# A hybrid decoder layer on one core: where the output projection ends, where the DeltaNet inverse's matmuls stand in the queue, which banks the gates use, and how GLA's output products are ordered

## The chip, the core and the metric

The kernel runs on one core of one Trainium2 chip. The core has five engines that work side by side, each with its own queue of instructions taken in order: PE (TensorE, matrix products), DVE (VectorE), ACT (ScalarE), POOL (GpSimd) and SP (SyncE, which here only issues transfers). Products land in PSUM, which has eight banks of 128 x 512 numbers. The metric is the device time of one execution in microseconds (us); lower is better.

## The reference

One layer of a decoder trunk, in float32, with 512 tokens behind 16 learned meta tokens and 2048 columns. The normalised input goes through one projection, whose columns are shared out to three token mixers; their outputs are gated, laid side by side and projected back. The mixers are a gated DeltaNet (6 heads of 128), GLA, a gated linear attention (5 heads, keys of 64, values of 128), and a forgetting attention, "fox" (5 heads of 128).

```python
h = concatenate([meta, x]);  proj = rms_norm(h, norm_w) @ w_in      # 528 x 7585
# DeltaNet, per chunk of 64 tokens: a_mat is strictly lower triangular
sol = triangular_solve(eye + a_mat, rhs, lower=True, unit_diagonal=True)
u, w = sol[..., :128], sol[..., 128:]
v_new = u - w @ s;  o = (q * exp(g)) @ s + qk @ v_new
s = s * g_last + k_dec.T @ v_new
# GLA, per chunk
o = (q * exp(g)) @ s + attn @ v;  s = g_last[:, None] * s + k_dec.T @ v
# both: o = rms(o) * w * silu(z);  fox: softmax(q k / sqrt(d) + c_t - c_s) v * silu(z)
o = concatenate([o_dn, o_gla, o_fox])[512 tokens]
y = x + o @ w_out                                                   # 2048 x 2048
out = rms_norm(y, final_norm_w)
```

## The kernel before, in words

**Exact splitting.** The two projections use TensorE's float32r form. Every operand is cut in two (`split`, L144 and L145: a cast hi on ScalarE, the rest lo = raw - hi on VectorE), and each product is three matmuls: hi hi, hi lo, lo hi. Weights come in pieces of 128 x 1024 (`load_half`: a load on SP's queue, then the split). The pool wp holds two buffers of each of raw, hi and lo, so that at most two pieces are under way, and a third waits until TensorE has finished with the first. The pool hp holds 32 tiles, first for the split input (xh, xl), at the end for the split outputs of the mixers (oh, ol), for weights kept back (wlh, wll) and for the final norm's weights (fw).

**PSUM.** Two pools of four banks each: psb (tag b) for the projections' accumulators, psm (tag m) for the mixers' small products.

**Order.** The program is written mixer by mixer, but a planner with its own costs merges everything into one fixed order for each engine; splits have high priority. So in the trace the mixers' small products stand among the input projection's matmuls (pp, L168: 128 x 128 weights against 264 or 256 tokens).

The four places that the change touches:

- *Gates.* 64 matmuls (L314) over the input's 16 row blocks give the narrow columns of all gates, for two halves of the tokens, in two accumulators pgate0 and pgate1 taken from psb. What follows adds two row halves and stores them in misc (L319 to L321).
- *The inverse.* DeltaNet works in two groups of three heads. `dn_inverse` inverts the 64 x 64 unit triangles of a group. The 32 x 32 diagonal blocks go by DMA into ab, one block in each of 51 partitions; thirty substitution steps of a multiply and an add on VectorE (L456, L458) invert them; POOL masks twice (L459, L461); a DMA on ScalarE's queue writes the result out (sc2, L464), two more read it back in another layout (iv at L467, xm at L469), and VectorE transposes (L471, L472). Then come 24 small matmuls pm (L478), a copy to m1 (L480), 48 small matmuls pl (L485, L486), and from them the next size up (pn L506, pu L511).
- *GLA's output.* `gla_pair` treats two heads (the last call one). For each head e and each block b of 128 tokens a product of 128 rows (at with vt, L769) and one of 64 rows (qd with the state ss, L770; head 0 uses rows 0 to 63, head 1 rows 64 to 127) add up in the same columns of the accumulator pgo. In the trace one such float32 product is two passes.
- *The output projection and the final norm.* The weight w_out has four column quarters cc of 512 and eight pieces kp, each for two of the sixteen heads i. For cc from 0 to 3 the first seven pieces are multiplied into four accumulators pa, one for each block tb of 128 tokens; for cc below 3 they are added to the residual at once (acc). The eighth piece of every quarter (heads 14 and 15) is kept back (`load_last`, rawl, wlh, wll) and multiplied in a last stage: for tb from 0 to 3 and for cc in the order 3, 0, 1, 2 six matmuls (pz, or pa for quarter 3), an add on VectorE (L972), a square with its sum on ScalarE (L974), and a multiply by fw on POOL (L976) for all but quarter 2. After a block's four quarters come the root (L978 to L980), the scaling of the quarters by ScalarE or VectorE (L984, L986, L988) and the writes, by SP's queue for even quarters and by ScalarE's for odd ones (L990).

Of the kernel before, what the change touches and what calls it, by code (L numbers as in the profile page):

```python
# [8 lines left out]
F32 = mybir.dt.float32  # L9
# [4 lines left out]
AF = mybir.ActivationFunctionType  # L14
ALU = mybir.AluOpType
# [3 lines left out]
P = 128  # L19
D = 2048  # L20
KT = D // P
NM = 16
S = 512
T = NM + S
HT = T // 2
NB = S // P
# [51 lines left out]
def tile_hybrid_trunk(ctx, tc, xT, xtok, mtok, w_gate, w_in, w_out, consts, lmask, fin_w, out, dbg=None):  # L78
    nc = tc.nc
# [19 lines left out]
    V, A, G, PE = nc.vector, nc.scalar, nc.gpsimd, nc.tensor  # L99
# [34 lines left out]
    def load_half(src, name):  # L134
        raw = wp.tile([P, 1024], F32, tag="raw", name=f"raw{name}")
        nc.sync.dma_start(out=raw, in_=src)
# [20 lines left out]
    def part(name, n=512):  # L157
        return hp.tile([P, T], F32R, tag="x", name=name)[:, :n]

    xh, xl = [], []  # L160
    rstd = cst.tile([P, T], F32, name="rstd")

    def inproj_part(ps, parts, k0, n, hi, lo, m=P):
        for j in range(n):
            k = k0 + j
            for wt, xx in ((hi, xh), (hi, xl), (lo, xh)):
                for p_, (t0, nt) in zip(ps, parts):
                    PE.matmul(p_[:, :nt], wt[:, j * m : (j + 1) * m], xx[k][:, t0 : t0 + nt],  # L168
                              start=(k == 0 and wt is hi and xx is xh),
                              stop=(k == KT - 1 and wt is lo))  # L170

    def inproj_begin(key, meta=True, first=0):
        b = BLOCK_OF[key]
# [69 lines left out]
    for b in range(5):  # L243
        r = NM if b == 4 else P
# [48 lines left out]
    zs = {}  # L293
# [13 lines left out]


    misc = cst.tile([64, T], F32, name="misc")
    pgate = [psb.tile([P, 512], F32, tag="b", name=f"pgate{a}") for a in range(2)]  # L310
    for k in range(KT):
        for xx in (xh, xl):
            for a in range(2):
                PE.matmul(pgate[a][:, :HT], wg[k // 8][:, k % 8, :], xx[k][:, a * HT : (a + 1) * HT],  # L314
                          start=(k == 0 and xx is xh), stop=(k == KT - 1 and xx is xl))
# [120 lines left out]
    def dn_inverse(g, st):  # L436
        an, anm = st["an"], st["anm"]
# [28 lines left out]
        xc, uc, m1, l1 = (iv[:, i] for i in range(4))  # L466
# [8 lines left out]
        for n in range(NN):  # L475
            for q in range(2):
                lo_, hi_ = slice(64 * q, 64 * q + 32), slice(64 * q + 32, 64 * q + 64)
                PE.matmul(pm[lo_, n, :], an[hi_, n, lo_], uc[hi_, n, :], start=True, stop=True)  # L478
# [160 lines left out]
    def gla_pair(p):  # L639
        R = P if p < 2 else 64  # L640
        ne = 2 if p < 2 else 1
# [121 lines left out]
            ss.append(sn)  # L763
        po = [psm.tile([P, 512], F32, tag="m", name=f"pgo{p}{e}") for e in range(ne)]
        for e in range(ne):
            rr = slice(64 * e, 64 * e + 64)
            for b in range(NB):
                bs = slice(b * P, (b + 1) * P)
                PE.matmul(po[e][:, bs], at[:, e * NB + b, :], vt[:, e, bs], start=True, stop=False)  # L769
                PE.matmul(po[e][:, bs], qd[rr, bs], ss[b][rr, :], start=False, stop=True)  # L770
# [123 lines left out]
    for h in range(FOX_HEADS):  # L894
        dump(f"ofx{h}", zs["fz", h])


    heads = [("dz", h) for h in range(DN_HEADS)] + [("gz", h) for h in range(GLA_HEADS)] \
        + [("fz", h) for h in range(FOX_HEADS)]
# [9 lines left out]
    def mms(p_, hi, lo, i, tb, first, last):  # L909
        s = slice(tb * P, (tb + 1) * P)  # L910
        oh, ol = oparts[i]
        for n, (o_, w_) in enumerate(((oh, hi), (oh, lo), (ol, hi))):
            PE.matmul(p_, o_[:, s], w_, start=(first and n == 0), stop=(last and n == 2))  # L913

    LAST = 14
    halves = lambda w: [[t[:, j * 512 : (j + 1) * 512] for t in w] for j in range(2)]
    acc, wl = {}, {}

    def load_last(c):
        raw = wp.tile([P, 1024], F32, tag="raw", name=f"rawl{c}")  # L920
        nc.sync.dma_start(out=raw, in_=w_out[c, LAST // 2])
        r = []
        for j in range(2):
            hi, lo = part(f"wlh{c}{j}"), part(f"wll{c}{j}")
            split(raw[:, j * 512 : (j + 1) * 512], hi, lo)
            r.append((hi, lo))
        return r

    for i in range(LAST):
        split_o(i)  # L930
    for cc in range(4):
        pa = [psb.tile([P, 512], F32, tag="b", name=f"pa{cc}{tb}") for tb in range(4)]
        for kp in range(LAST // 2):
            w = halves(load_half(w_out[cc, kp], f"o{cc}_{kp}"))
            for j in range(2):
                i = 2 * kp + j
                for tb in range(4):
                    mms(pa[tb], *w[j], i, tb, i == 0, cc < 3 and i == LAST - 1)
            if cc == 3 and kp % 2 and kp < 6:
                c = kp // 2  # L940
                wl[c] = load_last(c)
        for tb in range(4):
            if 4 * cc + tb < 11:
                a = zp.tile([P, S], F32, tag="zs", name=f"acc{cc}{tb}")
            else:
                a = six.tile([P, S], F32, tag="six", name=f"acc{cc}{tb}")
            nc.scalar.dma_start(out=a, in_=xtok[tb * P : (tb + 1) * P, cc * 512 : (cc + 1) * 512])
            if cc < 3:
                V.tensor_tensor(out=a, in0=a, in1=pa[tb], op=ALU.add)
            acc[tb, cc] = a  # L950
        if cc == 0:
            for i in range(LAST, KT):
                split_o(i)
    wl[3] = halves(load_half(w_out[3, LAST // 2], "l3"))
    fw = []
# [4 lines left out]
    ss = wk.tile([P, 4, 5], F32, tag="fss", bufs=1, name="fss")  # L960
    rr = wk.tile([P, 4], F32, tag="frs", bufs=1, name="frs")
    for tb in range(4):
        for cc in (3, 0, 1, 2):
            a = acc[tb, cc]
            cuts = 2 if (tb, cc) == (3, 2) else 1
            for n in range(cuts):
                c = slice(512 // cuts * n, 512 // cuts * (n + 1))
                p_ = pa[tb] if cc == 3 else psm.tile([P, 512], F32, tag="m", name=f"pz{tb}{cc}{n}")
                for j in range(2):
                    hi, lo = wl[cc][j]  # L970
                    mms(p_[:, c], hi[:, c], lo[:, c], LAST + j, tb, cc < 3 and j == 0, j == 1)
                V.tensor_tensor(out=a[:, c], in0=a[:, c], in1=p_[:, c], op=ALU.add)  # L972
                sq = row(f"sqf{tb}{cc}{n}")
                A.activation(sq[:, c], a[:, c], AF.Square, accum_out=ss[:, tb, cc + 2 * n : cc + 2 * n + 1])  # L974
            if cc != 2:
                G.tensor_tensor(out=a, in0=a, in1=fw[cc], op=ALU.mult)  # L976
# [4 lines left out]
        for cc in (3, 0, 1, 2):  # L981
# [64 lines left out]
```

## Time and profile before

| | |
|---|---|
| time, median of 3 runs | 1046.04 us (1045.03 to 1049.08) |
| profiled execution | 1048.64 us, of which the trace's span is 1046.9 us |
| TensorE busy | 97% of the span, 7787 matmul passes |
| VectorE, ScalarE, POOL busy | 55%, 39%, 13% |
| mean granted TensorE clock | 0.991 |
| memory traffic | 98.74 MB read, 5.05 MB written |

Rows of the profile have this form: line, engine, operation, out<-in by the program's names, partitions x elements, and "x" the count; times are in microseconds unless marked ns. What stands in brackets at the end of a row is how long the engine sat idle before it, and what ended that. PEclk is the clock that the throttle granted to TensorE (1.00, or 9 in the page's row of tenths, is full speed). Matmuls are pipelined: the distance from one start to the next, not the length of a row, is what a matmul costs.

### The profile page before, as it was taken

Reading aid. Unit: us, or ns where it says so; the run is one execution under the profiler, and the core shown is the slowest. Engines: PE = TensorE matmul, PEld = TensorE weight load, DVE = VectorE, ACT = ScalarE, POOL = GpSimd, SP = SyncE. Lnnn points to the kernel's source line nnn. Section 1 sums busy time; section 2 is a strip of 40 time slices with the busy share of each in tenths; the row PEclk is TensorE's granted clock in tenths of the full one; section 3 lists DMA queues with packets and bytes.
Section 4 is the critical chain, followed back from the end, with each engine's and each line's share of the span. In section 5 each row is a group of like instructions: output and inputs, shape, how many; then the busy total and the mean of one; then the engine's idle time right before and its main releaser. Section 6 shows DMA issues by size and latency. Waiting matters only on the chain.

```text
span 1046.9 us, 19027 instructions
## 1 busy us (share of the span) xinstructions
PE 1019.8 (97%) x7787; PEld 914.5 (87%) x7787; DVE 574.8 (55%) x1251; ACT 410.7 (39%) x895; POOL 134.9 (13%) x137
## 2 busy tenths in 40 slices
PE   9999999999999999999999999999999999999994
PEld 7899999989999888899989878898989888888883
DVE  6366868855567972334828274455444474332437
ACT  6643533343455333244344443333323262222234
POOL 0021312220213131000100010110101010000014
PEclk9999999999999998999999999999999999999998
DMA  9613222223222322222212122222222263222424
GB/s 351 233 48 127 82 89 92 99 77 108 89 69 82 96 102 77 69 77 73 78 42 67 46 87 74 94 72 86 89 84 87 86 204 126 93 82 100 141 81 160
DMA packets 42347, 105.15 MB, mean 100 GB/s; under 512 B 10589, under 2 KB 13917, under 8 KB 42260
## 3 DMA queue, kind: packets, MB, share of 16 engines
q1 hardware_dynamic: 26848, 90.23, 24.6%
q10 hardware_dynamic: 15412, 13.70, 4.5%
q8 instruction: 61, 1.00, 0.4%
q14 instruction: 26, 0.21, 0.1%
HBM read 98.74 MB, written 5.05 MB: 99 GB/s over the span
## 4 chain that ended last, share of the span: by engine, by line
PE 54%; DVE 3%; ACT 1%; issue 1%; DMA 0%; DVEq 0%
PE pp L168 29%; PE pa L913 15%; PE pss L708 1%; PE pgo L770 1%; PE pfo L863 1%; PE pgo L769 1%; PE pfa L831 1%; PE pz L913 1%; DVE acc L988 1%; PE pfx L846 1%; ACT sqf L974 0%; PE pfd L832 0%; PE pfo L866 0%; DVE acc L986 0%; PE pgk L660 0%
## 5 line engine op out<-in xcount | busy, mean ns | idle before, releaser
L168 PE MATMUL pp<-xh,whi 128*128 128x264 f32 (+2 forms) x1456 | 378.5, 312 | 0.9 <-DVE vg L278 0.8
L168 PE MATMUL pp<-xh,wlo 128*128 128x264 f32 (+2 forms) x1456 | 376.8, 311 | 0.0
L168 PE MATMUL pp<-xl,whi 128*128 128x264 f32 (+2 forms) x1456 | 376.2, 310 | 0.0
L168 PEld LDWEIGHTS pp<-xh,whi 128*128 128x128 f32 x1456 | 244.5, 190 | 16.0 <-issue 1.4
L168 PEld LDWEIGHTS pp<-xl,whi 128*128 128x128 f32 x1456 | 245.2, 190 | 14.4 <-issue 1.4
L168 PEld LDWEIGHTS pp<-xh,wlo 128*128 128x128 f32 x1456 | 245.4, 190 | 13.3 <-issue 0.3
L145 DVE TENSOR_TENSOR wlo<-raw,whi 128x1024 fp32r<-128x1024 f32 x110 | 136.4, 1240 | 124.6 <-ACT whi L144 123.8
L144 ACT CAST whi<-raw 128x1024 fp32r<-128x1024 f32 x110 | 115.3, 1049 | 202.2 <-PE pp L168 181.1
L913 PE MATMUL pa<-whio,ol 128*128 128x512 f32 x224 | 88.0, 393 | 0.0
L913 PE MATMUL pa<-wloo,oh 128*128 128x512 f32 x224 | 87.9, 393 | 0.0
L913 PE MATMUL pa<-whio,oh 128*128 128x512 f32 x224 | 79.1, 396 | 0.0
L145 DVE TENSOR_TENSOR wloo<-rawo,whio 128x1024 fp32r<-128x1024 f32 x28 | 34.6, 1236 | 75.2 <-ACT whio L144 75.1
L144 ACT CAST whio<-rawo 128x1024 fp32r<-128x1024 f32 x28 | 29.4, 1049 | 93.7 <-PE pa L913 60.1
L913 PEld LDWEIGHTS pa<-whio,ol 128*128 128x128 f32 x224 | 42.1, 188 | 9.9
L913 PEld LDWEIGHTS pa<-wloo,oh 128*128 128x128 f32 x224 | 42.1, 188 | 9.5
L913 PEld LDWEIGHTS pa<-whio,oh 128*128 128x128 f32 x224 | 42.0, 188 | 9.2
L287 POOL TENSOR_SCALAR stc<-cv 128x528 f32<-128x528 f32 (+1 forms) x18 | 28.3, 1572 | 165.3 <-DVE cv L361 142.5
L361 DVE SCALAR_TENSOR_TENSOR cv<-pb,cpk,cv 128x528 f32<-128x528 f32 (+1 forms) x54 | 40.8, 755 | 0.6
L976 POOL TENSOR_TENSOR acc<-acc,fw 128x512 f32<-128x512 f32 x12 | 15.7, 1335 | 170.9 <-ACT sqf L974 170.9
L278 DVE TENSOR_TENSOR pb<-pp,rstd 128x264 f32<-128x264 f32 (+1 forms) x36 | 13.8, 424 | 26.2 <-PE pp L168 26.1
L456 DVE TENSOR_TENSOR ot<-ab 51x30 f32<-51x30 f32 (+14 forms) x60 | 20.3, 339 | 3.3 <-POOL stc L287 1.7
L458 DVE TENSOR_TENSOR ab<-ab,ot 51x30 f32<-51x30 f32 (+14 forms) x60 | 20.6, 343 | 1.5
(380 smaller groups left out, 1304.2 us busy)
## 6 DMA issues: line engine op xcount, KB each, us to landing
raw<-in_w_in SPq DMA_DIRECT2D x110, 512.0 KB, 3.2
rawo<-in_w_out SPq DMA_DIRECT2D x28, 512.0 KB, 3.2
xt<-in_xtok SPq DMA_DIRECT2D x8, 512.0 KB, 9.1
acc<-in_xtok ACTq DMA_DIRECT2D x16, 256.0 KB, 5.4
xs<-in_xT SPq DMA_DIRECT2D x7, 528.0 KB, 6.8
rawl<-in_w_out SPq DMA_DIRECT2D x4, 512.0 KB, 5.2
out<-acc SPq DMA_DIRECT2D x8, 256.0 KB, 2.5
out<-acc ACTq DMA_DIRECT2D x8, 256.0 KB, 2.6
```

The costliest lines, as they stand in the source:

```text
L144: A.copy(hi, raw)
L145: V.tensor_tensor(out=lo, in0=raw, in1=hi.bitcast(F32), op=ALU.subtract)
L168: PE.matmul(p_[:, :nt], wt[:, j * m : (j + 1) * m], xx[k][:, t0 : t0 + nt], start=(k == 0 and wt is hi and xx is xh), stop=(k == KT - 1 an ...
L278: V.tensor_tensor(out=o, in0=p_[rows], in1=rstd[rows, t0 : t0 + n], op=ALU.mult)
L287: G.tensor_scalar_max(t, src, LOW)
L361: V.scalar_tensor_tensor(out=c, in0=pb[:, t0 + w : w + T], scalar=cwc[:, blk, w : w + 1], in1=c, op0=ALU.mult, op1=ALU.add)
L456: V.tensor_tensor(out=t3, in0=a3[:, j + 1 :, j : j + 1].to_broadcast([NN * 4 + H, m, j]), in1=a3[:, j : j + 1, 0:j].to_broadcast([NN * 4 + ...
L458: V.tensor_tensor(out=a3[:, j + 1 :, 0:j], in0=a3[:, j + 1 :, 0:j], in1=t3, op=ALU.add)
L708: PE.matmul(ps[o0 : o0 + n, b * n : b * n + n], kx[rr, k0 : k0 + n], qx[rr, q0 : q0 + n], start=True, stop=True)
L769: PE.matmul(po[e][:, bs], at[:, e * NB + b, :], vt[:, e, bs], start=True, stop=False)
L913: PE.matmul(p_, o_[:, s], w_, start=(first and n == 0), stop=(last and n == 2))
L976: G.tensor_tensor(out=a, in0=a, in1=fw[cc], op=ALU.mult)
```

## The change

Four parts.

1. The gates' two accumulators are taken from psm instead of psb. Since a tile's pool decides what it has to wait for, the planner may order the 64 matmuls anew.
2. The first pm matmul of each DeltaNet group is put behind a given matmul of the input projection (PM counts 308 and 310 projection matmuls on from where pm is written). This is an order for the planner alone; no semaphore is added. The planner then orders what follows, and in group 1 what leads to it, anew.
3. GLA's products: first all of 128 rows, head by head, then all of 64 rows, with the two heads taking turns in every block. Each accumulator is one group from the first product to the last.
4. The output projection: quarters 1 and 2 take all eight pieces at once; quarter 0 takes seven, and its eighth (as pb, in psm) after quarter 1. They are added and squared there. Quarter 3 takes five pieces for all tokens; its last three are kept (`load_last`) and multiplied in the last stage, 18 matmuls for each block of 128 tokens, for the last block in two column halves. POOL multiplies quarters 0 to 2 by fw before that stage's scaling, in the order of quarters. All writes go by SP's queue.

```diff
+    order, later = [], []
+    def behind(mm, n):
+        later.append((mm.ins, len(order) + n))
...
 def inproj_part(...):
+                    order.append(mm.ins)
...
-    pgate = [psb.tile([P, 512], F32, tag="b", name=f"pgate{a}") for a in range(2)]
+    pgate = [psm.tile([P, 512], F32, tag="m", name=f"pgate{a}") for a in range(2)]
...
-                PE.matmul(pm[lo_, n, :], an[hi_, n, lo_], uc[hi_, n, :], start=True, stop=True)
+                mm = PE.matmul(pm[lo_, n, :], an[hi_, n, lo_], uc[hi_, n, :], start=True, stop=True)
+                if n + q == 0:
+                    behind(mm, PM[g])
...
         for e in range(ne):
-            rr = slice(64 * e, 64 * e + 64)
             for b in range(NB):
-                PE.matmul(po[e][:, bs], at[:, e * NB + b, :], vt[:, e, bs], start=True, stop=False)
-                PE.matmul(po[e][:, bs], qd[rr, bs], ss[b][rr, :], start=False, stop=True)
+                PE.matmul(po[e][:, bs], at[:, e * NB + b, :], vt[:, e, bs], start=b == 0, stop=False, ...)
+        for b in range(NB):
+            for e in range(ne):
+                rr = slice(64 * e, 64 * e + 64)
+                PE.matmul(po[e][:, bs], qd[rr, bs], ss[b][rr, :], start=False, stop=b == NB - 1, ...)
...
+    PM = (308,310)
+    for mm, n in later:
+        tc.add_manual_dep(mm, order[n].name, ...NoSync..., reason="behind")
...
-    LAST = 14
+    FIRST, LAST = 14, 10
-    def load_last(c):                      # eighth piece of quarter c
+    def load_last(kp):                     # piece kp of quarter 3
...
     for cc in range(4):
+        n = (FIRST // 2, KT // 2, KT // 2, LAST // 2)[cc]
+        for kp in range(n):
+            run(pa, cc, kp, kp == 0, kp == n - 1)
+            if cc == 3 and kp >= 2:
+                load_last(kp + 3)
+        if cc == 3:
+            break
+        for tb in range(4):
+            add(tb, cc, pa[tb])
+            if cc > 0:
+                square(tb, cc)
+        if cc == 1:
+            pb = [psm.tile([P, 512], F32, tag="m", name=f"pb{tb}") for tb in range(4)]
+            run(pb, 0, FIRST // 2, True, True)
+            for tb in range(4):
+                add(tb, 0, pb[tb])
+                square(tb, 0)
...                                        # the four loads of fw, as before
+    for cc in range(3):
+        for tb in range(4):
+            weigh(tb, cc)                  # POOL: acc * fw
+    add(3, 3, pa[3], slice(256, 512))
     for tb in range(4):
-        for cc in (3, 0, 1, 2):            # six matmuls, add, square, multiply by fw
+        cuts = 2 if tb == 3 else 1
+        for n in range(cuts):
+            c = slice(512 // cuts * n, 512 // cuts * (n + 1))
+            p_ = psm.tile([P, 512], F32, tag="m", name="pz") if n else pa[tb]
+            for i in range(LAST, KT):
+                mms(p_[:, c], hi[:, c], lo[:, c], i, tb, n == 1 and i == LAST, i == KT - 1, ...)
+            add(tb, 3, p_, c)
+            square(tb, 3, c, n)
...                                        # sum, Ln, Exp as before
-            if cc == 0:
+            if cc % 2 == 0:
                 A.activation(a, a, AF.Copy, scale=r)
-            elif cc == 2:
+            elif cc == 3:
                 V.scalar_tensor_tensor(out=a, in0=a, scalar=r, in1=fw[cc], op0=ALU.mult, op1=ALU.mult)
...
-            q = nc.scalar if cc % 2 else nc.sync
-            q.dma_start(out=out[tb * P : (tb + 1) * P, cc * 512 : (cc + 1) * 512], in_=a)
+            nc.sync.dma_start(out=out[tb * P : (tb + 1) * P, cc * 512 : (cc + 1) * 512], in_=a)
```

More of the change, by code (lines that the diff above doesn't have):

```diff
@@ L167, in inproj_part @@
                 for p_, (t0, nt) in zip(ps, parts):
-                    PE.matmul(p_[:, :nt], wt[:, j * m : (j + 1) * m], xx[k][:, t0 : t0 + nt],
-                              start=(k == 0 and wt is hi and xx is xh),
-                              stop=(k == KT - 1 and wt is lo))
+                    mm = PE.matmul(p_[:, :nt], wt[:, j * m : (j + 1) * m], xx[k][:, t0 : t0 + nt],
+                                   start=(k == 0 and wt is hi and xx is xh),
+                                   stop=(k == KT - 1 and wt is lo))
+                    order.append(mm.ins)
     def inproj_begin(key, meta=True, first=0):
@@ L895, in tile_hybrid_trunk @@
         dump(f"ofx{h}", zs["fz", h])
+    for mm, n in later:
+        tc.add_manual_dep(mm, order[n].name, mybir.DependencyInfo(
+            mybir.DependencyClass.NoSync, mybir.DependencyReason.DATA), reason="behind")
     heads = [("dz", h) for h in range(DN_HEADS)] + [("gz", h) for h in range(GLA_HEADS)] \
@@ L907, in split_o, with mms @@
         oparts.append((hi, lo))
-    def mms(p_, hi, lo, i, tb, first, last):
+    def mms(p_, hi, lo, i, tb, first, last, **kw):
         s = slice(tb * P, (tb + 1) * P)
@@ L912, in mms @@
         for n, (o_, w_) in enumerate(((oh, hi), (oh, lo), (ol, hi))):
-            PE.matmul(p_, o_[:, s], w_, start=(first and n == 0), stop=(last and n == 2))
-    LAST = 14
+            PE.matmul(p_, o_[:, s], w_, start=(first and n == 0), stop=(last and n == 2), **kw)
+    FIRST, LAST = 14, 10
     halves = lambda w: [[t[:, j * 512 : (j + 1) * 512] for t in w] for j in range(2)]
     acc, wl = {}, {}
-    def load_last(c):
-        raw = wp.tile([P, 1024], F32, tag="raw", name=f"rawl{c}")
-        nc.sync.dma_start(out=raw, in_=w_out[c, LAST // 2])
-        r = []
+    def load_last(kp):
+        raw = wp.tile([P, 1024], F32, tag="raw", name=f"rawl{kp}")
+        nc.sync.dma_start(out=raw, in_=w_out[3, kp])
+        wl[kp] = []
@@ L923, in load_last, with add @@
         for j in range(2):
-            hi, lo = part(f"wlh{c}{j}"), part(f"wll{c}{j}")
+            hi, lo = part(f"wlh{kp}{j}"), part(f"wll{kp}{j}")
             split(raw[:, j * 512 : (j + 1) * 512], hi, lo)
-            r.append((hi, lo))
-        return r
-    for i in range(LAST):
+            wl[kp].append((hi, lo))
+    def add(tb, cc, p_, c=slice(0, 512)):
+        a = acc[tb, cc][:, c]
+        V.tensor_tensor(out=a, in0=a, in1=p_[:, c], op=ALU.add)
+    ss = wk.tile([P, 4, 5], F32, tag="fss", bufs=1, name="fss")
@@ new lines, in tile_hybrid_trunk, with square, weigh, run @@
+    rr = wk.tile([P, 4], F32, tag="frs", bufs=1, name="frs")
+    def square(tb, cc, c=slice(0, 512), n=0):
+        sq = row(f"sqf{tb}{cc}{n}")
+        A.activation(sq[:, c], acc[tb, cc][:, c], AF.Square, accum_out=ss[:, tb, cc + n : cc + n + 1])
+    def weigh(tb, cc):
+        G.tensor_tensor(out=acc[tb, cc], in0=acc[tb, cc], in1=fw[cc], op=ALU.mult)
+    def run(pa, cc, kp, first, last):
+        w = halves(load_half(w_out[cc, kp], f"o{cc}_{kp}"))
+        for j in range(2):
+            for tb in range(4):
+                mms(pa[tb], *w[j], 2 * kp + j, tb, first and j == 0, last and j == 1)
@@ L930, in tile_hybrid_trunk @@
+    for i in range(FIRST):
         split_o(i)
+    fw = []
     for cc in range(4):
[L932 to L941, printed above, removed]
@@ L942, in tile_hybrid_trunk @@
         for tb in range(4):
             if 4 * cc + tb < 11:
-                a = zp.tile([P, S], F32, tag="zs", name=f"acc{cc}{tb}")
+                acc[tb, cc] = zp.tile([P, S], F32, tag="zs", name=f"acc{cc}{tb}")
             else:
[L946 to L949, printed above, removed]
@@ L950, in tile_hybrid_trunk @@
-            acc[tb, cc] = a
+                acc[tb, cc] = six.tile([P, S], F32, tag="six", name=f"acc{cc}{tb}")
+            nc.scalar.dma_start(out=acc[tb, cc], in_=xtok[tb * P : (tb + 1) * P, cc * 512 : (cc + 1) * 512])
+        pa = [psb.tile([P, 512], F32, tag="b", name=f"pa{cc}{tb}") for tb in range(4)]
+        n = (FIRST // 2, KT // 2, KT // 2, LAST // 2)[cc]
[3 more added lines that the diff above has]
+                load_last(kp + 3)
@@ L951, in tile_hybrid_trunk @@
+        if cc == 3:
[4 more added lines that the diff above has]
+                square(tb, cc)
         if cc == 0:
-            for i in range(LAST, KT):
+            for i in range(FIRST, KT):
                 split_o(i)
-    wl[3] = halves(load_half(w_out[3, LAST // 2], "l3"))
-    fw = []
+        if cc == 1:
[4 more added lines that the diff above has]
+                square(tb, 0)
@@ L959, in tile_hybrid_trunk @@
         fw.append(f)
-    ss = wk.tile([P, 4, 5], F32, tag="fss", bufs=1, name="fss")
-    rr = wk.tile([P, 4], F32, tag="frs", bufs=1, name="frs")
+    for cc in range(3):
+        for tb in range(4):
+            weigh(tb, cc)
+    add(3, 3, pa[3], slice(256, 512))
     for tb in range(4):
-        for cc in (3, 0, 1, 2):
[L964 to L976, printed above, removed]
+        cuts = 2 if tb == 3 else 1
[3 more added lines that the diff above has]
+            for i in range(LAST, KT):
+                hi, lo = wl[i // 2][i % 2]
+                mms(p_[:, c], hi[:, c], lo[:, c], i, tb, n == 1 and i == LAST, i == KT - 1, skip_group_check=True)
+            add(tb, 3, p_, c)
+            square(tb, 3, c, n)
         r = rr[:, tb : tb + 1]
```

7 lines of the change are left out of this document (6 added, 1 removed).

## The prediction

> **What bounds the kernel now.** I read the page first (busy time by engine, the row of granted clock), then TensorE's waits, then the stretches around each wait, and last the rows of the four places that the diff touches.
>
> ```profile
> PE 1019.8 (97%) x7787; PEld 914.5 (87%) x7787; DVE 574.8 (55%) x1251; ACT 410.7 (39%) x895; POOL 134.9 (13%) x137
> PEclk9999999999999998999999999999999999999998
> ```
>
> TensorE (PE) is busy for 1019.8 of 1046.9 us, the next engine for 55%. So time comes off only where TensorE waits, where it runs slowly, or behind its last matmul. Its waits:
>
> ```profile
> PE pm L478 <- DVE iv L472: 4.4, 2, 2.2
> PE pss L708 <- issue: 3.9, 4, 1.3
> PE pgate L314 <- DVE zdz L299: 0.9, 1, 0.9
> ```
>
> Busy also hides slow running. By stretches (us; busy of PE, PEld, DVE, ACT, POOL; PEclk; DMA share; GB/s):
>
> ```profile
> 220.00:230.00 10.00, 8.07 (x181) 7.86 (x182) 6.75 (x13) 5.25 (x10) 1.20 (x1) 0.83 0.19 60
> 400.00:410.00 10.00, 9.55 (x181) 9.31 (x182) 2.88 (x7) 5.87 (x11) 0.21 (x1) 0.66 0.16 56
> 410.00:420.00 10.00, 10.00 (x58) 8.25 (x57) 3.65 (x8) 2.57 (x3) 1.39 (x1) 1.00 0.16 52
> ```
>
> The two stretches below 1.00 hold the two pm waits; the third stands for a stretch without one. Everything below is a sum against the profiled execution: 1048.64 us, of which 1046.9 is the span. The median of the runs, 1046.04, is 2.6 lower; I take the gains off that, since they are differences. About 0.5% (5 us) is what a measurement of this kernel tells from no change.
>
> **Part 1, the gates' banks.** The two pgate accumulators leave the pool psb for psm.
>
> ```profile
> 54.58 0.39 PE L314 MATMUL pgate<-xh,wg 128*128 128x264 f32 x1 [0.92 <-DVE zdz L299]
> ```
>
> TensorE waited 0.92 us for VectorE to free a psb bank. psm is empty then, so the wait goes; the adds it waited for are covered by the 64 gate matmuls. The next user of psb can be held up for a part at most: 0.5 to 0.9, I take **0.9**.
>
> **Part 2, the inverse's matmuls later.** The first pm matmul of a group gets an ordering behind a later projection matmul. In the built order of the changed kernel it is moved past 21 matmuls in group 0 and 31 in group 1.
>
> ```profile
> 221.93 0.95 PE L478 MATMUL pm<-iv,an 32*32 32x32 f32 x48 [2.23 <-DVE iv L472]
> 222.80 0.68 PE L168 MATMUL pp<-xh,whi 128*128 128x264 f32 x2
> 226.36 0.43 PE L168 MATMUL pp<-xh,wlo 128*128 128x264 f32 x2
> 226.62 0.40 PE L168 MATMUL pp<-xh,whi 128*128 128x264 f32 x2
> 226.86 0.40 PE L168 MATMUL pp<-xl,whi 128*128 128x264 f32 x2
> ...
> 397.84 0.40 PE L168 MATMUL pp<-xh,wlo 128*128 128x264 f32 x2
> 400.44 1.49 PE L478 MATMUL pm<-iv,an 32*32 32x32 f32 x48 [2.21 <-DVE iv L472]
> 401.86 0.81 PE L168 MATMUL pp<-xh,whi 128*128 128x264 f32 x2
> 407.31 0.41 PE L168 MATMUL pp<-xh,whi 128*128 128x264 f32 x2
> 408.25 0.21 PE L485 MATMUL pl<-iv 32*32 32x32 f32 x1
> ```
>
> A pair of pp matmuls takes 0.244 us at full clock (226.62 to 226.86), 0.122 each. From 222.80 to 226.36 eight pairs take 3.56 us instead of 1.95: 1.6 lost to the clock. From 401.86 to 407.31 twelve pairs take 5.45 instead of 2.93, and pm itself 1.49 instead of 0.95: 3.1 lost. So each stall of 2.2 us drags a half clock behind it; the two places cost 3.8 and 5.3 us.
>
> Group 0: the moved matmuls cover 21 x 0.122 = 2.56 us of a 2.23 us wait; nothing ahead of it changes on any queue, so all 3.8 come off. The margin is 0.3 us.
>
> Group 1: 31 x 0.122 = 3.78 us would cover 2.21 with 1.6 to spare, but the planner also re-ordered what leads to it.
>
> ```profile
> 386.95 0.69 DVE L291 TENSOR_TENSOR zsgz<-zgz,stgz 128x512 f32<-128x512 f32 x1 [0.81 <-ACT stgz L290]
> 387.77 0.18 DVE L458 TENSOR_TENSOR ab<-ab,ot 51x30 f32<-51x30 f32 x1
> 387.88 1.22 DVE L145 TENSOR_TENSOR wlo<-raw,whi 128x1024 fp32r<-128x1024 f32 x1
> 391.59 0.26 ACTq L464 DMA_DIRECT2D sc<-ab  x1
> 396.93 0.38 ACTq L467 DMA_DIRECT2D iv<-sc  x1
> 399.81 0.58 DVE L472 STREAM_TRANSPOSE iv<-iv 128x384 f32<-128x384 f32 x1 [5.27 <-DMA iv<-sc]
> ```
>
> Before, one substitution step is left behind zsgz at 386.95 and the subtract wlo (1.22) comes after the last. In the changed order four and a half steps are left behind zsgz, and the subtract stands among them: nine small instructions (0.18 the last, the earlier ones longer: I take 0.25) and 1.22 us from 387.6 on, so the last step ends near 391.1 instead of 387.95. POOL's masking up to the DMA out, that DMA and the DMA back keep their distances (3.6, 5.3 and 2.9 us), the next zsgz stands just ahead of the transpose (some 0.2), and from there to pm it is 0.6 as before: pm is ready near 403.7 instead of 400.4. TensorE arrives at 398.1 + 3.8 = 401.9. So a wait of about 1.8 us remains (1.0 to 2.4). Whether it halves the clock the trace does not settle: 2.2 us did twice, the waits of up to 1.3 us in the list above did not. I put half weight on one lost spell of 1.7 us (0.17 of the 10 us in the row 220 to 230). Group 1 costs 1.8 + 0.9 = 2.7 instead of 5.3. Behind pm, pl is moved too, and the copies it needs come about 1 us before TensorE does. Part 2: 3.8 + 2.6 = **6.4**, from 3.8 (group 1 gains nothing) to 9.1 (no wait is left).
>
> A rule of the Trainium skill speaks against this part: "TensorE: Matmul & The Clock Gate", Part 1, says the clock goes to half after at least one idle window of about 3.4 us and counts busy-ness in a free-running window. By it a 2.2 us stall alone would not have halved anything, which the rows above contradict unless the tiny pm matmuls count as idle too; that reading is a rival below.
>
> **Part 3, GLA's output grouped.** Products over 128 rows and over 64 rows alternate before; after, all of the first stand together, then all of the second.
>
> ```profile
> 590.03 0.38 PE L769 MATMUL pgo<-gvt,kq 128*128 128x128 f32 x2
> 590.34 0.49 PE L770 MATMUL pgo<-gs,gqd 64*128 64x128 f32 x2
> 596.17 0.48 PE L770 MATMUL pgo<-gsn,gqd 64*128 64x128 f32 x2
> 596.59 0.39 PE L168 MATMUL pp<-xh,wlo 128*128 128x264 f32 x1
> ```
>
> and from the chain of waits (start, us, what), two runs of products of one shape:
>
> ```profile
> 439.22 0.67 PE py L584 x6
> 587.49 0.81 PE pgn L759 x12
> ```
>
> A full pair of heads takes 590.03 to 596.59, 6.56 us for 16 products of two passes (x2), 0.41 each. Products of one shape in a row take 0.112 us a pass (py) or 0.068 (pgn), so two passes take 0.22 at most and a change of shape costs 0.19. After: 16 passes of L769 by 0.112, 1.8; 16 of L770 by 0.068 to 0.112, 1.1 to 1.8; two changes of shape, 0.4. That is 3.3 to 4.0 for 6.56. Five heads of four blocks make 20 products on each of the two lines, so there are two and a half such pairs: 2.5 x (2.6 to 3.3) = 6.4 to 8.2, I take **7.4**. The least is 3.8: if going between the two row halves (L770's heads alternate between rows 0-63 and 64-127) costs what a change of shape does, only L769 gains, 20 x 0.19.
>
> "TensorEngine Tiling (Array Packing)", Key Properties, in the Trainium skill says that different tiles can work in parallel, up to twice the rate for two row halves; by that L770 would take 0.9 a pair and the part would bring 8.6.
>
> **Part 4, the output projection's end.** Before, columns of all four quarters end in the last stage, and VectorE, ScalarE and POOL lag.
>
> ```profile
> 1029.69 0.39 PE L913 MATMUL pz<-wll,oh 128*128 128x512 f32 x1
> 1031.31 0.39 PE L913 MATMUL pz<-wlh,ol 128*128 128x512 f32 x1
> 1033.51 0.28 PE L913 MATMUL pz<-wlh,ol 128*128 128x256 f32 x1
> 1017.26 7.96 POOL L976 TENSOR_TENSOR acc<-acc,fw 128x512 f32<-128x512 f32 x6 [163.43 <-ACT sqf L974]
> 1039.45 0.40 ACT L974 ACTIVATE sqf<-acc 128x256 f32<-128x256 f32 x1
> DMA to landing us min/median/max: 3.1/3.7/4.3
> 1005.10 1.05 ACT L144 CAST whio<-rawo 128x1024 fp32r<-128x1024 f32 x1 [7.80 <-DMA rawo<-in_w_out]
> L136 SPq DMA_DIRECT2D rawo<-in_w_out x28: 327/328/328, 831.7 to 998.4; - x28
> ```
>
> The last matmul ends at 1033.8, the last half square starts at 1039.45, the span ends at 1046.9: 13.1 us, of which 7.45 (square, sum, root, scaling, write) run from that square's start in any case. After, three quarters are summed and squared while TensorE works, and behind the last matmul stand one half add (I take the 0.40 of the half square for it, 0.6 with the hand-overs) and the 7.45: 8.0 at best. The count of matmuls is the same (0.231 us each: 7 steps in 1.62).
>
> What can hold it: POOL's 12 multiplies, 1.33 us each by the row of six (7.96), 15.9. They wait for fw, issued on ScalarE's queue behind the last weight cast. That cast needs the buffer of the fourth of the last quarter's eight weight pairs, so it comes 4 x 24 x 0.231 = 22.2 us into the quarter's 44.4; fw has landed by some 26.5 (landings of 3.1 to 4.3, the row without a time), they end near 42.5, 2 us ahead of the last matmul. But ScalarE's queue is in order: its scaling of acc20 waits for the ninth multiply and stands ahead of the squares of the next token block; working that off costs about 1 us at the end. So 9.1 instead of 13.1: 4.0, and a 0.43 us stall inside the old last stage goes: **4.4** (2.4 to 5.5).
>
> All 16 writes now go by SP's queue; it has no loads left by then.
>
> **Sum.** 0.9 + 6.4 + 7.4 + 4.4 = 19.1: the profiled execution would go to 1029.5, the median to **1027**. The bounds together: 0.5 + 3.8 + 3.8 + 2.4 = 10.5 and 0.9 + 9.1 + 8.2 + 5.5 = 23.7, so 1035 to 1022.
>
> **Rivals.** (a) The pm wait moves along: the chain to it is VectorE, POOL and two DMAs, so if group 0's margin of 0.3 us is missed as well, the half clock stays twice and part 2 brings 0.5: gain 13.2, **1033**. For it: the delay found in group 1. Against: group 0's order is unchanged. Chance 0.12. (b) The end does not shorten: fw lands late or POOL runs slower beside VectorE, and ScalarE's queue is held to the end. POOL has 2 us to spare. Gain 14.7, **1031**; 0.10. (c) The half clock comes from the tiny matmuls and not from the stall: it stays with the stall gone. That takes 1.6 and 2.2 (3.1 less the 0.9 kept) from my sum: gain 15.3, **1031**. Against it: the pl matmuls, of the same size, run from 408.25, and the stretch 410 to 420 shows 1.00. 0.05. (The Trainium skill's page on the clock gate, Part 1, as cited, would make this the likelier reading.) (d) Slower: the last quarter must fetch eight weight pairs, and three of them are held for the end, all through two raw buffers. If those act as one, a pair costs landing + cast 1.05 + subtract 1.22. The last of the 28 loads was issued at 998.4 and its cast began at 1005.10, 6.7 us: 9.0 a pair against TensorE's 24 x 0.231 = 5.5, 3.5 us of gap, and 1.7 of half clock behind each: 8 x 5.2 = 41, less the other 14.7: **1072**. It decides from a landing near 5.1, where eight gaps of 1.8 eat the 14.7. Against: with two buffers a load lands under the pair before, and TensorE did not wait for the late one (its list of waits has no pa). 0.07, of which 0.02 for a mild form that ends within 0.5%.
>
> **Chances.** Forecast 0.66, rivals 0.12, 0.10, 0.05, 0.07. 1022 to 1035 takes in the forecast's bounds and (a) to (c). Faster by over 0.5%: 0.93; within: 0.02; slower: 0.05.
>
> **What would show it.** No pgate wait; pm waits near 0 and 1 to 2 us, granted clock 1.00 in the first place; pgo of a pair in 3 to 4 us; last matmul to end in 8 to 10 us, POOL done before the last matmul. Wrong if TensorE waits for wlh or whio in the last 45 us, or if pm waits 2 us twice.

## The result, and the profile after

The changed kernel takes 1034.51 us (median; 1033.69 to 1035.39), the kernel before in the same comparison 1049.01 us. The ratio is 0.9869, 95% interval 0.9849 to 0.9889: 1.3% faster. The profiled execution took 1035.39 us, with a span of 1033.7. Forecast were 1027 and a gain of 19.1 us; the medians differ by 14.5 and the profiled executions by 13.2. (The forecast started from 1046.04, a median of three runs; the six runs of this comparison put the kernel before at 1049.01.)

Where it came from can be read off ScalarE's weight casts (L144). The first 110 whole-piece casts (128 x 1024) prepare the input projection's weights and are the same in both traces; most of them wait for TensorE to give a buffer back, so they mark how far TensorE has come. The start of the n-th of them, in us:

| | before | after | difference | change since the line above |
|---|---|---|---|---|
| first cast | 47.46 | 46.59 | -0.87 | -0.9 (nothing of the change runs before it) |
| 13th, behind the gates | 131.98 | 129.94 | -2.04 | -1.2: part 1 |
| 52nd, behind group 0 of the inverse | 392.23 | 390.44 | -1.79 | +0.2: part 2 |
| 61st, behind group 1 | 475.20 | 473.82 | -1.38 | +0.4: part 2 |
| 101st, behind GLA | 777.06 | 769.30 | -7.76 | -6.4: part 3 |
| end of the span | 1046.9 | 1033.7 | -13.2 | -5.4: part 4 |

Three parts brought what was forecast, within about a microsecond. Part 2, for which 6.4 us were in the sum, cost 0.6. The page after, and TensorE's waits:

```profile
PE 1011.4 (98%) x7799; PEld 910.3 (88%) x7799; DVE 566.7 (55%) x1240; ACT 411.7 (40%) x899; POOL 136.4 (13%) x137
PE pss L717 <- issue: 3.5, 3, 1.4
PE pm L485 <- DVE iv L479: 3.0, 1, 3.0
PE pn L515 <- DVE uf L504: 2.3, 1, 2.3
```

The pgate wait is gone. One pm wait is gone and the other has grown from 2.2 to 3.0 us, and pn, which stands two products behind pm (pm, pl, pn), waits 2.3 us: 5.3 us of waits for 4.4. The clock went with them (columns as in the prediction's rows of stretches):

```profile
220.00:230.00 10.00, 9.78 (x205) 9.13 (x203) 5.50 (x11) 5.14 (x9) 1.92 (x3) 1.00 0.18 54
230.00:240.00 10.00, 7.80 (x68) 7.50 (x69) 7.25 (x15) 4.14 (x7) 0.00 (x0) 0.83 0.21 60
400.00:410.00 10.00, 6.97 (x71) 6.42 (x70) 3.60 (x7) 6.21 (x10) 1.30 (x2) 0.67 0.29 74
```

The clock is full where group 0's pm now runs (220 to 230), and the same 0.83 stands ten microseconds later, at pn.

**Group 0.** TensorE, ScalarE and VectorE in the timeline of the changed kernel (start, length, engine, line, [idle before <- releaser]):

```profile
220.31 0.95 PE L485 MATMUL pm<-iv,an 32*32 32x32 f32 x48
232.20 1.08 PE L515 MATMUL pn<-uf,an 64*64 64x64 f32 x12 [2.33 <-DVE uf L504]
...
228.75 0.65 ACT L295 ACTIVATE stc<-stc 128x528 f32<-128x528 f32 x1 [4.41 <-POOL pb L363]
230.11 0.64 ACT L297 ACTIVATE stc<-stc 128x528 f32<-128x528 f32 x1
230.78 0.48 ACT L496 COPY iv<-pl 128x384 f32<-128x384 f32 x1
...
231.34 0.71 DVE L504 COPY uf<-iv 32x384 f32<-32x384 f32 x2 [4.31 <-ACT iv L496]
```

pm starts with no wait. But the planner has put the three activations of a silu (stc, L295 to L297) ahead of the copy of pl (L496) on ScalarE's queue. The first of them waits 4.41 us for POOL. So the copy, whose data were there before 226 (pl's last matmul starts at 225.20), runs at 230.78, the copies uf follow on VectorE, and pn waits for them. In the kernel before, the copy of pl stood ahead of the silu:

```profile
228.50 0.48 ACT L487 COPY iv<-pl 128x384 f32<-128x384 f32 x1 [2.53 <-PE pl L486]
230.52 0.65 ACT L288 ACTIVATE stc<-stc 128x528 f32<-128x528 f32 x1 [1.54 <-POOL stc L287]
```

**Group 1.**

```profile
387.81 1.21 DVE L145 TENSOR_TENSOR wlo<-raw,whi 128x1024 fp32r<-128x1024 f32 x1
389.92 0.18 DVE L465 TENSOR_TENSOR ab<-ab,ot 51x30 f32<-51x30 f32 x1
392.80 0.26 ACTq L471 DMA_DIRECT2D sc<-ab  x1
399.48 0.38 ACTq L474 DMA_DIRECT2D iv<-sc  x1
401.99 0.69 DVE L298 TENSOR_TENSOR zsgz<-zgz,stgz 128x512 f32<-128x512 f32 x1 [8.16 <-ACT stgz L297]
403.23 1.40 PE L485 MATMUL pm<-iv,an 32*32 32x32 f32 x48 [3.02 <-DVE iv L479]
```

The subtract wlo stands among the substitution steps, and the last step ends at 390.1. By the table this kernel is 1.8 us ahead here, so that is 391.9 on the times of the kernel before, 3.9 later than there (forecast 391.1). POOL's masking takes 2.7 us from there to the DMA out, 3.6 before; the DMA out takes 6.7 us to where the DMA back is issued, 5.3 before; and zsgz stands ahead of the transpose. The wait is 3.0 us, forecast 1.8.

**GLA** (two rows of the chain of waits: start, us, what; then two of the timeline) and the **end**:

```profile
534.47 1.78 PE pgo L777 x16
536.25 1.09 PE pgo L783 x16
...
534.31 1.95 PE L777 MATMUL pgo<-gvt,kq 128*128 128x128 f32 x16
537.28 0.39 PE L174 MATMUL pp<-xh,whi 128*128 128x264 f32 x1
...
1004.68 15.69 POOL L959 TENSOR_TENSOR acc<-acc,fw 128x512 f32<-128x512 f32 x12 [158.57 <-DMA fw<-in_fin_w]
1025.13 0.28 PE L932 MATMUL pz<-wlh,ol 128*128 128x256 f32 x1
1026.37 0.40 ACT L956 ACTIVATE sqf<-acc 128x256 f32<-128x256 f32 x1
```

The two groups of a pair of heads take 2.87 us together; from the first product to the next projection matmul it is 2.97 (534.31 to 537.28), for 6.56 before. The last matmul ends at 1025.4 and the span at 1033.7: 8.3 us for 13.1, with POOL's multiplies over at 1020.4.

### The profile page after: what moved, and what is told of

The parts are those of the page before. It is cut to its first block, busy times and chain, and to the rows that moved or that the text cites. A ratio compares the mean times of both kernels' runs of the same rounds, so it can differ in the third digit from the quotient of the medians.

```text
span 1033.7 us, 19032 instructions
## 1 busy us (share of the span) xinstructions
PE 1011.4 (98%) x7799; PEld 910.3 (88%) x7799; DVE 566.7 (55%) x1240; ACT 411.7 (40%) x899; POOL 136.4 (13%) x137
## 4 chain that ended last, share of the span: by engine, by line
PE 66%; DVE 5%; DMA 3%; issue 3%; ACT 2%; POOL 1%; ACTq 0%; POOLq 0%; DVEq 0%
PE pp L174 39%; PE pa L932 15%; DMA sc<-ab 1%; PE pss L717 1%; POOL stgz L294 1%; DVE wlo L145 1%; PE pfo L877 1%; PE pfa L845 1%; PE py L593 1%; PE pb L932 1%; PE pfx L860 1%; DVE ab L465 1%; PE po L608 1%; PE po L607 1%; PE pa L570 0%
## 5 line engine op out<-in xcount | busy, mean ns | idle before, releaser
L174 PEld LDWEIGHTS pp<-xh,wlo 128*128 128x128 f32 x1456 | 245.2, 190 | 13.1 <-issue 0.2
L144 ACT CAST whi<-raw 128x1024 fp32r<-128x1024 f32 x110 | 115.4, 1049 | 202.3 <-PE pp L174 175.3
L144 ACT CAST whio<-rawo 128x1024 fp32r<-128x1024 f32 x29 | 30.4, 1049 | 83.8 <-PE pa L932 56.8
```

The lines of the kernel that those rows point to most:

```text
L144: A.copy(hi, raw)
L174: mm = PE.matmul(p_[:, :nt], wt[:, j * m : (j + 1) * m], xx[k][:, t0 : t0 + nt], start=(k == 0 and wt is hi and xx is xh), stop=(k == KT - ...
```

## The experiments

The theory after this reading: the ordering of pm moves its waits along, because the planner re-orders ScalarE and VectorE behind it and ahead of it. The rival: the ordering does bring some 6 us, and something that arises with the other parts takes them back.

**One part alone, or all but one.** e1_pm_alone is the kernel before with part 2 only; e2_without_pm is the changed kernel without it; e3_gla_alone has part 3 only, e4_end_alone part 4 only. Their edits are the pieces of the diff above; e1's is

```diff
+                if n + q == 0:
+                    behind(mm, PM[g])
```

with `behind`, `order`, PM and the loop over `later`.

> Only the pm ordering is put into the kernel before. If the waits merely move (theory: pn waits 2.3 us in group 0, pm 3.0 us in group 1, each with a half clock behind it), the time stays within 1.5 us of the kernel before and its trace shows both waits. If the ordering brings the 6.4 us of the prediction and the loss arises only together with the other parts, it is 4 to 8 us faster.

> The whole change without the pm ordering. If the pm ordering brings nothing, this is as fast as the whole change: 12 to 14 us faster than the kernel before, with the two old pm waits of 2.2 us in the trace. If the ordering is worth 6.4 us, this is only 7 to 8 us faster.

> Only the grouping of GLA's products. By the alignment of the weight casts in the two traces 6.3 us faster (5.5 to 7.0), a pair of heads in some 4.0 us instead of 6.6. If the gain in that stretch came from something else (fewer waits of the mixers' small products after the new order), 1 to 3 us faster.

> Only the new output projection. By the alignment of the casts 5.4 us faster (4.5 to 6.0): last matmul to end 8.3 us instead of 13.1 and no 0.43 us wait. If ScalarE's queue is held by POOL without the other parts, under 3 us.

| | ratio to the kernel before | 95% interval |
|---|---|---|
| e1_pm_alone | 1.0017 | 0.9999 to 1.0035 |
| e2_without_pm | 0.9878 | 0.9846 to 0.9909 |
| e3_gla_alone | 0.9941 | 0.9920 to 0.9961 |
| e4_end_alone | 0.9951 | 0.9931 to 0.9972 |

Part 2 alone brings nothing, and the change without it is as fast as with it: the rival falls. Without the ordering the two old pm waits are back, 4.8 us in all in e2's profile. Parts 3 and 4 alone bring 6.2 and 5.1 us of 1049, close to the casts' 6.4 and 5.4. The waits of e1_pm_alone stand at the places of the changed kernel's, without its other parts; that of pm is longer, 4.1 us for 3.0:

```profile
PE pm L485 <- DVE iv L479: 4.1, 1, 4.1
PE pn L515 <- DVE uf L504: 2.2, 1, 2.2
```

In the profile of e3_gla_alone the two groups of a pair take 2.88 us, as in the changed kernel (some 4.0 had been expected), and in that of e4_end_alone the last matmul ends 8.1 us before the span does (1030.92 + 0.28 to 1039.3).

**The order on ScalarE, group 0.** e5_copy_first is the changed kernel with one edge more for the planner:

```diff
-        A.activation(t, t, AF.Exp, scale=-1.0)                # in the silu
+        first[name] = A.activation(t, t, AF.Exp, scale=-1.0)
...
-        A.copy(l1, pl)                                        # in dn_inverse
+        l1_ = A.copy(l1, pl)
+        if g == 0:
+            after.append(("c10", l1_))
...
+    for x, y in after:
+        tc.add_manual_dep(first[x].ins, y.ins.name, ...NoSync..., reason="first")
```

> The whole change, and for group 0 one more edge: the first silu activation of block 10 stands behind the copy of pl on ScalarE's queue. If that order is why pn waits, the pn wait of 2.3 us and its half clock are gone: group 1 is unchanged, so 2.3 to 4.0 us less than the changed kernel, 0.983 to 0.985 of the kernel before. If the pn wait has another cause (the copies uf on VectorE, or pl itself too late), the time stays at 0.987.

0.9838 (0.9810 to 0.9865), 1032.16 us. The pn wait is gone, and the group's stretch runs at full clock:

```profile
225.90 0.48 ACT L496 COPY iv<-pl 128x384 f32<-128x384 f32 x1 [1.08 <-PE pl L495]
229.29 0.65 ACT L295 ACTIVATE stc<-stc 128x528 f32<-128x528 f32 x1 [2.91 <-POOL pb L363]
229.66 0.91 PE L517 MATMUL pn<-uf,an 64*64 64x64 f32 x12
```

The copy runs at 225.90 instead of 230.78, and pn without a wait. By the casts, the stretch from the 25th to the 52nd is 3.6 us shorter than in the kernel before, where the changed kernel's is 0.2 longer; forecast for a group 0 without a wait were 3.8. The cause of the pn wait is shown. (The ratio's interval still touches that of the changed kernel; the trace decides here.)

**Group 1 as well.** e6_both_mended adds to e5:

```diff
+        last[g] = st_                          # st_: the add of a substitution step
...
-    PM = (308,310)
+    PM = (308, 330)
...
+    after.append(("w29_0", last[1]))           # the subtract behind the last step
```

> As e5, and in group 1 the subtract of piece 29_0 stands behind the last substitution step, and pm is put 20 matmuls further back. If each wait has the cause that the trace names, no pm or pn wait over 1 us is left and the clock is full up to the end: 6 to 9 us less than the changed kernel, 0.979 to 0.982 of the kernel before. If the waits only move on to pl, pn or pu, 0.983 to 0.988.

0.9797 (0.9768 to 0.9826), 1028.35 us, clear of the changed kernel's interval.

```profile
PE pm L486 <- DVE iv L480: 1.6, 1, 1.6
386.88 0.18 DVE L465 TENSOR_TENSOR ab<-ab,ot 51x30 f32<-51x30 f32 x1
391.73 0.26 ACTq L472 DMA_DIRECT2D sc<-ab  x1
397.37 0.38 ACTq L475 DMA_DIRECT2D iv<-sc  x1
399.88 0.69 DVE L298 TENSOR_TENSOR zsgz<-zgz,stgz 128x512 f32<-128x512 f32 x1 [9.31 <-ACT stgz L297]
400.00:410.00 10.00, 8.88 (x176) 7.39 (x177) 5.01 (x10) 5.91 (x10) 0.00 (x0) 1.00 0.34 107
```

A pm wait of 1.6 us is left, more than the 1 us expected. The clock stays full here (1.00), which is luck in part: the wait fell across the border of two clock windows (last section). It is not full up to the end, as had been expected: a half spell of 3.4 us begins at 564.6, behind a wait of 1.4 us at pss.

This run made two edits in group 1 at once, and the trace tells them apart. The push back brought the gain: in the trace pm stands 12 projection matmuls further back than in the changed kernel, 12 x 0.122 = 1.5 us, and the wait is 1.4 us shorter. The edge brought pm's data no earlier in this execution: the last step ends about 0.9 us sooner (four projection matmuls of 0.23 us), but from there to pm it takes 14.1 us, 13.1 in the changed kernel. The DMA out is quicker (5.6 us), and the two maskings are slower, 4.5 us for 2.5, since the new edge puts one subtract wlo directly ahead of the first, and another runs ahead of the second. In all twelve traces the maskings that began while a subtract wlo was running on VectorE took 2.1 to 2.3 us each, and the others 1.26 or 1.55.

**Cover on TensorE alone.** e7_pushed_back leaves ScalarE and VectorE as the planner has them and only pushes the waiting matmuls further back: pn of group 0 by 25 matmuls, and pm of group 1 by 32 in PM's count, which makes 24 in the trace.

> The whole change with both matmul groups pushed further back on TensorE alone: pn of group 0 by 25, pm of group 1 by 32 matmuls; nothing is done about ScalarE's or VectorE's order. If cover on TensorE is all that is missing, as fast as e6. If the planner's answer to each push brings a new wait behind it, 0.983 to 0.988 and a wait of 1 to 2 us at pn, pu or ps.

0.9834 (0.9808 to 0.9861). No wait of pm or pn over 0.5 us is left, but

```profile
401.92 0.50 PE L174 MATMUL pp<-xh,whi 128*128 128x512 f32 x1 [0.89 <-ACT whi L144]
404.13 0.50 PE L174 MATMUL pp<-xh,wlo 128*128 128x512 f32 x1 [1.47 <-DVE wlo L145]
```

the projection itself now waits for its weights' split, which stands behind the DMA issues on ScalarE and the transposes on VectorE, and a half spell of 6.8 us follows. That is the outcome expected if the planner's answer brings a new wait, at another place than I named.

**Two versions further.** e9_mended_further takes e6, puts pm three matmuls further back and zsgz behind the subtract of piece 30_0; e11_two_queues is e9 with ScalarE's queue for the odd quarters of the last token block.

> As e6, with pm of group 1 three matmuls further back and the last silu product (zsgz of block gz4) behind the subtract of piece 30_0 on VectorE, so that the transposes come first. If that product is what still held pm 0.6 us, the remaining pm wait goes from 1.6 to about 0.7 us and the time is 0 to 1.5 us below e6, 0.978 to 0.980 of the kernel before. If the subtract now comes late for the next piece, a wait of pp for wlo of about 0.5 to 1 us takes the gain back.

> As e9, with the odd quarters of the last token block written by ScalarE's queue, as the kernel before does. If four issues on one queue delay the last write, the stretch from the last matmul to the end goes from 8.3 to 7.5 to 8.0 us; if the landing itself takes the time, it stays at 8.3.

0.9812 (0.9784 to 0.9840) and 0.9811 (0.9787 to 0.9835): neither can be told from e6 by time. In e9's profile pm waits 1.4 us in two places, the longest 1.2 (0.7 had been expected), no wait for wlo appears, and there is no half-speed spell before the last matmul. In e11's profile the pm wait is 2.5 us, though the order is the same: from the issue of the DMA out to that of the DMA back it takes 7.2 us, in e9 5.7, so a cover that is just long enough in one execution is not in the next. From the last matmul to the end e11 takes 7.9 us and e9 8.4. That is within what was expected of two queues, but the other traces with all writes on one queue show 8.1 to 9.5, so one execution of each does not settle it. The three are the fastest versions found, about 2% below the kernel before and 0.6% below the changed kernel in their medians.

**Row halves.** e8_heads_in_turn is the changed kernel with GLA's 64-row products head by head.

```diff
-        for b in range(NB):
-            bs = slice(b * P, (b + 1) * P)
-            for e in range(ne):
+        for e in range(ne):
+            for b in range(NB):
+                bs = slice(b * P, (b + 1) * P)
```

> The whole change with GLA's 64-row products head by head instead of alternating between the row halves. If the two row halves work side by side, the 64-row part of a pair becomes slower (from 1.8 us or less to about 3); if not, the same 1.8 us, and the same time within the scatter.

```profile
536.11 1.78 PE pgo L777 x16
537.89 1.64 PE pgo L783 x16
```

1.64 us instead of 1.09 for the same 16 passes. So of the 3.6 us that a pair gains, alternating between the row halves brings 0.55, and the rest comes with the grouping by shape; the slower form was expected at about 3 us and measured less. (There is one run of it, so its time of 1036.74 us is not compared.)

## Where the prediction was right, and where it was wrong

**What bounds the kernel** was right: TensorE is at 98% after, and each gain is a wait of TensorE, slow products on it, or the end.

**Part 1**, 0.9 forecast: 1.2 by the casts, and the same 1.15 in e2_without_pm. The wait was the whole of it (0.92 us and two short ones beside it, 1.17 in all), and the second user of psb held nothing up.

**Part 2** is the step that failed: 6.4 forecast, -0.6 measured, and it alone is more than the whole miss of 5.9 us between sum and profile. Two sentences of it were wrong.

- "nothing ahead of it changes on any queue, so all 3.8 come off." What stands ahead of pm is indeed unchanged and pm did not wait. But the sentence follows group 0 only as far as pl and the copies before it. The copy behind pl had been put behind a silu on ScalarE, visible in the built order, and pn paid 2.3 us and a half clock for it. e5 shows the 3.8 to be right once that one edge is restored (3.6).
- For group 1 the delay of the substitution was found in the order and sized at 3.1 us; it was 3.9, the DMA out took 1.3 longer, and the masking 0.9 less, so these did not "keep their distances". A wait of 3.0 was left, not 1.8, and the clock halved for 6.8 us. Half weight on one lost 1.7 us was too little: at 3.0 us the clock halved in every trace, and for two windows, 3.4 us lost. (The 1.3 us of the DMA is in part chance: e5, with group 1 unchanged, shows 5.8 us for it instead of 6.7.)

Rival (a), the wait moves along, gave 1033 and a gain of 13.2, which is what the profiled execution shows. That it agrees to the tenth is luck, since it put part 2 at +0.5, part 3 at 7.4 and part 4 at 4.4. Its mechanism was right only in part: group 0's margin of 0.3 us held, and the wait came back two products later. It had a chance of 0.12; having found one re-ordering ahead of group 1, I should have followed each queue past pn and pu in both groups, and raised that chance.

Rival (b), the end does not shorten, falls with part 4 below. Rival (c), the half clock comes from the tiny matmuls, falls as the cause that starts it: in the changed kernel the clock is 1.00 from 220 to 230, with all of group 0's pm and pl in it, and in e6 from 400 to 410. (They do seem to prolong it; see the last section.) The Trainium skill ("TensorE: Matmul & The Clock Gate", Part 1) speaks of at least one idle window of 3.4 us; here 2.2 us were enough when they lay in one window.

**Part 3**, 7.4 forecast: 6.4 by the casts, 6.2 alone. The price of 0.19 us for a change of shape holds for the order before: with e8's 1.64 us for the 64-row passes, (6.56 - 1.78 - 1.64) / 16 is 0.20. The two changes that remain, 0.4 in the sum, hardly show (2.97 for 2.87), and passes went by 0.111 (1.78 for 16) and 0.068 (1.09 for 16), the lower end that I had allowed. A pair therefore takes 2.97, less than the 3.3 to 4.0 of the sum. From first to last start in the two traces, without the projection matmuls between, the two pairs take 3.4 and 3.6 us less and the single head 1.2: 8.2 in all. Of that, the casts show 6.4. TensorE's waits in that stretch are 1.4 us longer, of which 0.8 at pkd, which waits for VectorE (1.1 us for 0.3), and 0.5 at pg, which waits for ScalarE and did not before: what the slow products had hidden. That leaves 0.4 us unexplained. In the other traces with this order the same stretch gains 4.8 to 7.7 us; the least are e5 and e6, which have a half spell in it.

**Part 4**, 4.4 forecast: 5.4. The end took 8.3 us, close to the 8.0 given as the best case; the microsecond for ScalarE's queue behind the ninth multiply was not needed. (In e2 and e5, with the same end, it is 9.5 and 9.2, so the 8.3 is one draw.) POOL began at 1004.7, soon enough to be 5 us ahead of the last matmul, where I had 2.

**Rival (d)**, late weights in the last quarter, did not show: no wait for wlh or whio is among those of the last 45 us.

## What to carry to other kernels

An instruction that is moved takes the planner's whole order with it, so follow the dependent chain on every in-order queue to its end, not to the next product; the first queue on which an unrelated instruction has stepped ahead is where the wait comes back. Where a wait has been moved and not shortened, try the order on the engine that delivers, and see in the trace whether the data come sooner: in group 0 one edge was worth 3.9 us by the casts, in group 1 another brought nothing by itself, as POOL became slower beside it. Pushing the consumer back has its own price: in e7 the weights' split came late instead. And price products of unlike row counts by how often the shape changes, not by their size.

## What the runs showed of the hardware

**The half clock comes in units.** Before the last matmul, the half-speed spells of every profile last 3.41 or 6.83 us, by the granted clock in the trace. In the kernel before the second begins 177.5 us after the first, 52 times 3.413; in the changed kernel it is 170.7, 50 times. So there is a fixed grid of windows, and a spell fills one or two of them. What decides is, for the most part, how much of one window TensorE is idle:

| run, wait | idle in the fuller window, us | clock after it |
|---|---|---|
| before, pm, 2.2 (both) | 2.2 | half |
| changed, pn, 2.3 | 2.3 | half |
| e2_without_pm, pm, 2.5 | 1.7 of 2.5 | half |
| e3_gla_alone, pp, 1.7 | 1.7 | half |
| e1_pm_alone, pss, 1.55 | 1.55 | half |
| e4_end_alone, pm, 2.2 | 1.5 of 2.2 | full |
| e4_end_alone, pm, 2.3 | 1.1 of 2.3 | full |
| e8_heads_in_turn, pn, 2.3 | 1.3 of 2.3 | full |
| e6_both_mended, pss, 1.4 | 1.4 | half |
| before, pss, 1.3 | 1.3 | full |
| e6_both_mended, pm, 1.6 | 1.25 of 1.6 | full |
| before, gates, 0.9 and two short ones | 1.2 | full |
| e4_end_alone, gates, the same | 1.2 | half |
| e5_copy_first, pss, 1.1 | 1.2 | half |

```profile
400.41 0.95 PE L478 MATMUL pm<-iv,an 32*32 32x32 f32 x48 [2.20 <-DVE iv L472]
400.00:410.00 10.00, 9.59 (x199) 9.01 (x200) 4.02 (x10) 6.91 (x12) 0.19 (x1) 1.00 0.18 56
```

These two rows are e4_end_alone's: the same wait of 2.2 us as in the kernel before, and a clock of 1.00 instead of 0.66, as the wait fell across the border of two windows (the grid follows from this run's one earlier spell, which begins at 55.0).

Over all twelve traces, from 45 us on and outside spells, each of the 16 windows with 1.55 us or more of idle time is followed by a half spell, and none with less than 1.15. Of the 21 windows from 1.17 to 1.50 three are. So the limit lies near 1.5 us of 3.4, but not sharply. (Ends of matmuls are modelled in the trace, and tiny products count as busy here.)

Whether a wait of 2 us costs 2 or up to 5.5 us is then a matter of where it falls in an execution. Pn's wait of 2.3 us in the changed order cost 3.9 us in the changed kernel's profile and 2.4 in e8's, by the casts from the 25th to the 52nd against e5's. That the window is free-running is what the Trainium skill's page on the clock gate, Part 1, says too; that an idle window must be whole is not borne out. The 3.8 and 5.3 us that the prediction read off one execution were therefore a draw of this lottery: of the four traces that leave pm where it was, the kernel before and e3 show these two spells, e2 one window less, and e4 neither.

**Long spells hold pm.** Of the 20 spells before the last matmul seven last two windows, and these are the seven in whose first window 44 or more of pm's 48 passes run; the other 13 have at most 14. So the tiny products did not start a half clock, but they went with a longer one each time. No run isolates this.

**The two row halves of the array work side by side**, as far as these two orders show: 16 passes of 64 rows take 1.09 us when they alternate and 1.64 when the four products of a half follow each other, half as much again and not twice.
